# Hybrid encoder step: four split weight blocks kept in DRAM by each layer's first group and loaded whole by the later groups

## The chip, the cores and the metric

The kernel runs on one core of one Trainium2 chip. The metric is device time in microseconds (us) of one execution. The kernel before was timed three times: 2314.01 us in the median, from 2313.35 to 2318.27. One more execution was profiled; all rows of the trace come from that one.

## The reference, cut to what matters

Two layers over 2048 prompt tokens and 8 x 16 sample tokens, model width 1024. Per layer:

```python
xn = rms_norm(h, norm_g)
u = xn @ w_in                                   # 1024 x 2832
qa, ka, va, ga, qb, kb, vb, gb, ab = jnp.split(u, _split_points(), axis=-1)
# A: sliding-window attention of qa, ka, va;  B: gated linear attention of qb, kb, vb, ab
mix = jnp.concatenate([oa * jax.nn.silu(ga), ob * jax.nn.silu(gb)], axis=-1)
h = h + mix @ w_out                             # 1024 x 1024
gate = jax.nn.sigmoid(rms_norm(h, pe_norm_g) @ w_pg)
h = h + gate * (p_l @ w_pe)                     # 256 x 1024
```

All tensors are float32.

## The kernel before

The 2176 tokens are 17 tiles of 128, in five groups of 3, 4, 4, 3 and 3 tiles; the last group holds the sample tokens. Each layer goes through the groups in turn, so that the execution has ten stretches, called group 0 to group 9 here; groups 0 and 5 are the first of their layers. A group runs phase_in (projections, attention, linear attention) and then phase_out (output projection, gate, embedding).

To keep float32 accuracy, each weight and each activation is split into a high part, rounded to the type fp32r, and a low part, the rest; a product is three matmuls (lines 400 to 402). The activations of a group are split once. The weights don't stay on the chip: every group loads them all again and splits them again.

The list plan holds the weight blocks in the order of their use, group by group: kv, q, ga0, ga1, qb, kb, vb, gb, o0 to o3, then g0, e0 to g3, e3. A block of 256 columns (ga0, ga1, qb, kb, o, g) has two slots of half its 1024 rows; q, vb and gb, of 512 columns, and kv have four slots. A slot is a tile named w of 128 partitions by 2 (high, low) by 1024 values, 8 KB on each partition, 1 MB in all; five slots exist in a ring. A piece is 256 rows of 256 columns (272 for kv), 256 KB; every slot of the four blocks is filled from two pieces. For each piece SyncE issues a DMA into one of four buffers named raw (line 197), ScalarE copies raw to the high part (line 217), and VectorE subtracts the high part from raw into the low part (line 96 through a helper). There are 800 pieces in an execution, 80 for each group.

w_split emits the next piece: it takes a slot from the ring if the piece needs one and one is free, and emits the raw DMAs up to four pieces ahead. It is called while the last unit of matmuls of a block gives its slots back (freed, end=True), and ahead of units (w_ahead). The raw DMA of piece i + 4 waits for the subtraction of piece i; the copy of a piece into a reused slot waits for the last matmul that reads what was in it. All instructions of an engine run in one order that is fixed when the program is built, and a waiting instruction holds up those behind it. All weight loads, the loads of the activations, cache and state, and the outputs are issued by SyncE in one order too.

In phase_in, units of 24 matmuls go to one PSUM buffer each. For ga, qb and kb a unit is 128 columns of the weights by all tokens of the group (512 or 384); for kv, q, vb and gb it is one tile of tokens by all columns. Evictions: q by VectorE at line 470 after a sum of squares (464, 466), ga at 761 with 751 and 752 for silu, qb at 780, kb at 784, vb by ScalarE at 1070. From the start of ga on, steps of attention and linear attention (scores s at 125 and 131, softmax at 571 to 590, transposes at 637 to 640, outputs o) are put between the units. The q tiles are transposed (546) and copied by ScalarE (548) before the scores; the gate of the linear attention runs at the same time (lines 1105 to 1117, with a table load ahead of the logarithm at 1112). The end of a group's linear attention is at lines 895 to 915.

Of the kernel before, what the change touches and what calls it, by code (L numbers as in the profile page):

```python
# [8 lines left out]
F32 = mybir.dt.float32  # L9
# [37 lines left out]
def hybrid_step(ctx: ExitStack, tc: tile.TileContext, a: dict, o: dict):  # L47
    nc = tc.nc
    V, A, G, PE, SP = nc.vector, nc.scalar, nc.gpsimd, nc.tensor, nc.sync
# [4 lines left out]
    dram = ctx.enter_context(tc.tile_pool(name="dram", bufs=1, space=bass.MemoryType.DRAM))  # L54
# [40 lines left out]
    def ptt(out, in0, in1, op1, eng=None):  # L95
        (eng or G).tensor_tensor(out=out, in0=in0, in1=in1, op=op1)  # L96
# [45 lines left out]
    plan = []  # L142
    for l in range(DEPTH):
        for gi in range(len(GROUPS)):
# [8 lines left out]
            for b in range(4):  # L153
                plan.append((l, gi, f"g{b}", 8, [a["w_pg"][l, :, b]], 4, "w"))
                plan.append((l, gi, f"e{b}", 2, [a["w_pe"][l, :, b]], 2, "we"))
    RING = dict(w=5, we=2)
    pieces = []
    for bi, (_, _, _, K, srcs, ks, _) in enumerate(plan):
        for k0 in range(0, K, 2):
            c0 = 0  # L160
            for src in srcs:
                wd = src.shape[2]
                pieces.append((bi, k0 // ks, k0 % ks, c0, wd, src[:, k0:k0 + 2, :]))
                c0 += wd
    first_piece = {}
    last_piece = {}
# [6 lines left out]
    st = dict(dma=0, split=0, blk=0)  # L173
    wgate = [None]
    RAW = Z["raw"]
# [17 lines left out]
    def w_dma(upto):  # L193
        while st["dma"] < min(upto, len(pieces)):
            bi, _, _, _, wd, src = pieces[st["dma"]]
            r = w_p.tile([128, 2, wd], F32, tag="raw", name="raw", bufs=RAW)
            SP.dma_start(out=r, in_=src)
            raws[st["dma"]] = r
            st["dma"] += 1

    def w_split():
        i = st["split"]
        if i >= len(pieces):
            return False
        bi, si, kk, c0, wd, _ = pieces[i]
        _, _, _, _, srcs, ks, tag = plan[bi]
        if (bi, si) not in slots:
            if held[tag] == RING[tag]:
                return False
            held[tag] += 1  # L210
            slots[bi, si] = w_p.tile([128, 2, ks, sum(x.shape[2] for x in srcs)], F32R, tag=tag, name="w", bufs=RING[tag])
        w_dma(i + RAW)
        w = slots[bi, si]
        r = raws.pop(i)
        hi, lo = (w[:, x, kk:kk + 2, c0:c0 + wd] for x in range(2))
        with tc.issue_after(wgate[0]) if wgate[0] is not None else ExitStack():
            A.activation(out=hi, in_=r, func=ACTF.Copy)  # L217
        ptt(lo, r, hi, ALU.subtract, V)
        st["split"] += 1
        w_dma(i + 1 + RAW)  # L220
        return True

    def w_get(l, gi, nm):
        bi = st["blk"]
        assert plan[bi][:3] == (l, gi, nm), (plan[bi][:3], l, gi, nm)
        while st["split"] <= last_piece[bi]:
            assert w_split()
        st["blk"] += 1
        return Block(bi)

    def w_get_part(l, gi, nm):

        bi = st["blk"]
        assert plan[bi][:3] == (l, gi, nm), (plan[bi][:3], l, gi, nm)
        while st["split"] < first_piece[bi] + 2:
            assert w_split()
        st["blk"] += 1
        return Block(bi)

    def w_rest(w):  # L240
        while st["split"] <= last_piece[w.bi]:
            assert w_split()
# [95 lines left out]
    def prep_x(pool, l, gi, slot, out, whole=False):  # L338
# [6 lines left out]
        if whole:  # L345
            full = pool.tile([128, KD, n], F32, tag="hfull", name="hfull", bufs=1)
            for k in range(0, KD, 2):
                HQ[k // 2].dma_start(out=full[:, k:k + 2, :], in_=src[:, k:k + 2, t0:t0 + n])
                if k // 2 in WD:
                    w_dma(WD[k // 2])  # L350
# [85 lines left out]
    def phase_in(l, gi, ip, xn, mslot, S_in):  # L436
# [651 lines left out]
        for mt in range(4):  # L1088
            if mt == 3:
                with tc.issue_after(lastmm[0]):  # L1090
                    done["tail"]()
            pss.append(unit_a(mixes, ws[mt // 2], mt % 2, 0, n, pm(n) if mt < 2 else pw1(n), ks=(0, 4), end=mt % 2 == 1))
        ws.append(w_get_part(l, gi, "o2"))
        for mt in (4, 5):
            pss.append(unit_a(mixes, ws[2], mt % 2, 0, n, pw1(n), ks=(0, 4), end=mt % 2 == 1))
# [176 lines left out]
def _prepare(inputs):  # L1272
# [65 lines left out]
    for t in range(NT):  # L1338
# [18 lines left out]
             ks=(DEPTH, 128, 128), vs=(DEPTH, 128, 128), ss=(DEPTH, 8, 128, 2, 128))  # L1357
# [32 lines left out]
```

## Time and profile before

| | us |
|---|---|
| median of three runs | 2314.01 |
| lowest, highest | 2313.35, 2318.27 |
| profiled execution | 2322.44 |
| its span, first to last instruction | 2320.7 |
| mean granted TensorE clock in the span | 0.993 |

The page gives for each engine the time in which it is busy, for the whole span and in 40 slices. Matmuls overlap, and a busy stretch of TensorE (PE) may hold matmuls that run slowly; the weight loads of TensorE are listed apart (PEld). DVE is VectorE, ACT is ScalarE, POOL is GpSimd, SP is SyncE, and SPq is its DMA-issuing side. The chain that ended last follows the execution back from its last instruction, at each step to what released it. The granted clock is a share of full speed: 1.00 is 2.4 GHz, and the lower level is 1.2 GHz.

In rows by group of instructions, names are output<-input. In rows of a timeline the first number is the start in us from the span's start, the second the duration in us of the instruction or of the run of equal instructions (x2 is two of them), and brackets give the engine's idle time ahead of it and what ended that.

### The profile page before, as it was taken

To read this page: it belongs to the slowest core of one execution; us is meant where nothing else is said; L and a number is where in the kernel's file an instruction comes from. 1 tells how busy PE (TensorE), PEld (TensorE's weight loads), DVE (VectorE), ACT (ScalarE), POOL (GpSimd) and SP (SyncE) were. 2 spreads that over 40 slices of the span, in tenths; PEclk is the share of its full clock that TensorE was granted. 3 is DMA by queue.
4 is the path that set the end of the run, shared out by engine and by line. 5 is a ranking of instruction groups with operands and counts; after the bars stand their busy time and mean duration, and the time that the engine had idled before them with its cause. 6 is when DMAs were issued, how large, how long until landed. Compare 5 with 4: busy or idle time off the path is not lost.

```text
span 2320.7 us, 40960 instructions
## 1 busy us (share of the span) xinstructions
PE 2268.3 (98%) x14814; PEld 1953.6 (84%) x14814; DVE 1605.0 (69%) x3279; ACT 1272.2 (55%) x2962; POOL 671.0 (29%) x771
## 2 busy tenths in 40 slices
PE   8999999999999999999999999999999999999999
PEld 7889877887788989987988998778877888798889
DVE  7767765767567766776777677657676678677755
ACT  6555644655455645654665566445555556566533
POOL 3124322342223231413322241314412142233222
PEclk9999999999999999999999999999999999999999
DMA  5344313433154425444543543244322443264343
GB/s 159 101 150 133 107 55 119 143 105 91 55 155 120 128 85 169 147 118 127 180 128 91 171 136 90 68 128 133 114 73 74 146 146 110 85 184 146 104 131 102
DMA packets 160234, 278.93 MB, mean 120 GB/s; under 512 B 17648, under 2 KB 43632, under 8 KB 160032
## 3 DMA queue, kind: packets, MB, share of 16 engines
q1 hardware_dynamic: 159344, 275.43, 39.4%
q8 instruction: 117, 1.92, 0.3%
q10 hardware_dynamic: 688, 0.88, 0.1%
q14 instruction: 85, 0.70, 0.1%
HBM read 255.41 MB, written 20.71 MB: 119 GB/s over the span
## 4 chain that ended last, share of the span: by engine, by line
PE 83%; ACT 4%; DVE 4%; DMA 4%; issue 3%; POOL 2%; ACTq 0%; DVEq 0%; POOLq 0%; SPq 0%
PE mm L400 15%; PE mm L402 15%; PE mm L401 14%; PE pw L400 9%; PE pw L401 9%; PE pw L402 9%; PE o L131 3%; DVE w L96 2%; PE s L131 2%; PE s L125 2%; DMA raw<-in_w_pe_dram 1%; DMA raw<-in_w_out_dram 1%; PE o L125 1%; ACT gsq L895 1%; ACT w L217 1%
## 5 line engine op out<-in xcount | busy, mean ns | idle before, releaser
L96 DVE TENSOR_TENSOR w<-raw,w 128x512 fp32r<-128x512 f32 (+1 forms) x800 | 571.7, 743 | 164.6 <-ACT w L217 161.7
L217 ACT ACTIVATE w<-raw 128x512 fp32r<-128x512 f32 (+1 forms) x800 | 468.9, 627 | 271.1 <-DMA raw<-in_w_pe_dram 60.0
L96 POOL TENSOR_TENSOR ot<-gth,hst 128x384 f32<-128x384 f32 (+1 forms) x79 | 101.7, 1291 | 287.6 <-DVE gth L1189 263.4
L400 PE MATMUL mm<-B,w 128*128 128x384 f32 (+1 forms) x440 | 160.8, 365 | 1.1 <-DVE yq L470 0.8
L402 PE MATMUL mm<-B,w 128*128 128x384 f32 (+1 forms) x440 | 159.8, 363 | 0.0
L401 PE MATMUL mm<-B,w 128*128 128x384 f32 (+1 forms) x440 | 159.0, 361 | 0.0
L400 PE MATMUL pw<-mix,w 128*128 128x384 f32 (+1 forms) x424 | 153.0, 361 | 0.0
L580 ACT ACTIVATE P<-s,mx 128x192 f32<-128x192 f32 (+3 forms) x272 | 108.8, 413 | 77.5 <-DVE mx L575 71.3
L401 PE MATMUL pw<-mix,w 128*128 128x384 f32 (+1 forms) x424 | 151.2, 357 | 0.0
L402 PE MATMUL pw<-mix,w 128*128 128x384 f32 (+1 forms) x424 | 151.0, 356 | 0.0
L400 PE MATMUL mm<-A,w 128*128 128x384 f32 (+1 forms) x408 | 148.5, 364 | 2.0 <-DVE yq L470 1.8
L96 POOL TENSOR_TENSOR acc<-sq,acc 128x384 f32<-128x384 f32 (+1 forms) x60 | 74.1, 1235 | 257.1 <-ACT sq L331 257.1
L402 PE MATMUL mm<-A,w 128*128 128x384 f32 (+1 forms) x408 | 148.0, 363 | 0.0
L401 PE MATMUL mm<-A,w 128*128 128x384 f32 (+1 forms) x408 | 147.8, 362 | 0.0
L400 PE MATMUL mm<-w,A 128*128 128x512 f32 (+1 forms) x360 | 138.2, 384 | 0.0
L400 PE MATMUL mm<-w,B 128*128 128x512 f32 (+1 forms) x360 | 137.9, 384 | 0.0
L402 PE MATMUL mm<-w,B 128*128 128x512 f32 (+1 forms) x360 | 137.7, 383 | 0.0
L402 PE MATMUL mm<-w,A 128*128 128x512 f32 (+1 forms) x360 | 137.6, 382 | 0.0
L401 PE MATMUL mm<-w,A 128*128 128x512 f32 (+1 forms) x360 | 137.4, 382 | 0.0
L401 PE MATMUL mm<-w,B 128*128 128x512 f32 (+1 forms) x360 | 137.4, 382 | 0.0
L96 POOL TENSOR_TENSOR mix<-ga_t,mix 128x512 fp32r<-128x512 f32 x34 | 43.9, 1290 | 283.1 <-ACT mix L606 283.1
L1186 ACT ACTIVATE gth<-gth 128x384 f32<-128x384 f32 (+2 forms) x81 | 45.1, 560 | 125.6 <-DVE gth L1185 125.3
(325 smaller groups left out, 6367.6 us busy)
## 6 DMA issues: line engine op xcount, KB each, us to landing
raw<-in_w_in_dram SPq DMA_DIRECT2D x400, 256.0 KB, 2.9
raw<-in_w_out_dram SPq DMA_DIRECT2D x160, 256.0 KB, 3.1
raw<-in_w_pg_dram SPq DMA_DIRECT2D x160, 256.0 KB, 2.9
raw<-in_w_in_dram SPq DMA_DIRECT2D x40, 272.0 KB, 3.2
raw<-in_w_pe_dram SPq DMA_DIRECT2D x40, 256.0 KB, 3.4
hl<-in_h_dram SPq DMA_DIRECT2D x24, 192.0 KB, 3.1
hbuf<-ot SPq DMA_DIRECT2D x24, 192.0 KB, 2.1
hx<-hbuf SPq DMA_DIRECT2D x24, 192.0 KB, 3.6
```

Source lines behind the costliest of these rows:

```text
L96: (eng or G).tensor_tensor(out=out, in0=in0, in1=in1, op=op1)
L125: prev[0] = PE.matmul(**kw).ins
L131: prev[0] = PE.matmul(**kw).ins
L217: A.activation(out=hi, in_=r, func=ACTF.Copy)
L400: PE.matmul(out=out, lhsT=sh, rhs=mh, start=first and i == 0, stop=False)
L401: PE.matmul(out=out, lhsT=sh, rhs=ml, start=False, stop=False)
L402: lastmm[0] = PE.matmul(out=out, lhsT=sl, rhs=mh, start=False, stop=last and i == n).ins
L580: A.activation(out=P[:, e, p0:p0 + wd], in_=ps[:, e // 2, e % 2, :wd], func=ACTF.Exp, scale=0.125, bias=mx[:, e:e + 1], accum_out=den[:, 0 ...
L895: A.activation(out=gq, in_=po[:, h % 2, h // 2, :], func=ACTF.Square, accum_out=ss[:, h:h + 1])
L1186: ta = A.activation(out=th[:, c], in_=th[:, c], func=ACTF.Tanh, scale=0.5)
```

## The change

In the first group of each layer, the slots of ga1, qb, kb and vb (2 + 2 + 2 + 4 = 10 slots) are filled as before, and after the last subtraction of a slot SyncE stores the whole slot, both parts, to a DRAM tile: 1 MB, 8 KB in a row for each partition. In the four later groups of the layer, each of these slots is one entry in the list of pieces, of width 0; for it w_split issues one DMA of 1 MB from the DRAM tile into the slot, with no raw buffer, no copy and no subtraction. The other blocks are loaded and split in every group as before.

```diff
     RING = dict(w=5, we=2)
+
+    KEEP = [('ga1','qb','kb','vb')]
+    kept = {}
+    for bi, (l, gi, nm, K, srcs, ks, _) in enumerate(plan):
+        if gi < len(KEEP) and nm in KEEP[gi]:
+            kept[l, nm] = (gi, dram.tile([K // ks, 128, 2, ks, sum(x.shape[2] for x in srcs)], F32, name=f"k{l}{nm}"))
     pieces = []
-    for bi, (_, _, _, K, srcs, ks, _) in enumerate(plan):
+    for bi, (l, gi, nm, K, srcs, ks, _) in enumerate(plan):
+        if (l, nm) in kept and gi > kept[l, nm][0]:
+            pieces += [(bi, si, 0, 0, 0, kept[l, nm][1][si]) for si in range(K // ks)]
+            continue
         for k0 in range(0, K, 2):
...
     def w_dma(upto):
         while st["dma"] < min(upto, len(pieces)):
             bi, _, _, _, wd, src = pieces[st["dma"]]
+            if not wd:
+                st["dma"] += 1
+                continue
...
         w_dma(i + RAW)
         w = slots[bi, si]
+        if not wd:
+            SP.dma_start(out=w.bitcast(F32), in_=src)
+            st["split"] += 1
+            w_dma(i + 1 + RAW)
+            return True
         r = raws.pop(i)
...
         st["split"] += 1
         w_dma(i + 1 + RAW)
+        if kept.get((l_, nm_), (None,))[0] == gi_ and (i == last_piece[bi] or pieces[i + 1][1] != si):
+            SP.dma_start(out=kept[l_, nm_][1][si], in_=w.bitcast(F32))
         return True
```

w_get_part, which asks for the first slot of a block, asks for one entry instead of two where the block is loaded whole; it is called for o2 alone, which isn't.

## Rows read from the trace of the kernel before

**Rows 1.** The page's first part (busy time and share of the span by engine) and its fourth (the chain that ended last, by engine).

```profile
PE 2268.3 (98%) x14814; PEld 1953.6 (84%) x14814; DVE 1605.0 (69%) x3279; ACT 1272.2 (55%) x2962; POOL 671.0 (29%) x771
...
PE 83%; ACT 4%; DVE 4%; DMA 4%; issue 3%; POOL 2%; ACTq 0%; DVEq 0%; POOLq 0%; SPq 0%
```

**Rows 2.** Busy time of each engine from the first eviction of ga to the last of vb in the eight later groups, and the sum. Columns: the stretch, its length, busy us (instructions) by engine, granted clock, mean share of the DMA engines, GB/s.

```profile
271.00:351.00 80.00, 80.00 (x558) 62.25 (x558) 56.37 (x122) 43.16 (x127) 16.46 (x21) 1.00 0.23 66
...
sum 569.00, PE 568.87 PEld 463.67 DVE 411.30 ACT 318.13 POOL 117.52; mean PE 71.11 PEld 57.96 DVE 51.41 ACT 39.77 POOL 14.69
```

**Rows 3.** Timeline of TensorE in group 2, from the last units of q to the first of ga0.

```profile
528.67 0.39 PE L401 MATMUL mm<-A,w 128*128 128x512 f32 x1
528.90 0.39 PE L402 MATMUL mm<-A,w 128*128 128x512 f32 x1
...
531.99 0.50 PE L400 MATMUL mm<-A,w 128*128 128x512 f32 x1 [1.85 <-DVE yq L470]
...
533.03 0.63 PE L400 MATMUL mm<-A,w 128*128 128x512 f32 x1
533.46 0.63 PE L401 MATMUL mm<-A,w 128*128 128x512 f32 x1
```

**Rows 4.** Timeline of VectorE at the same place.

```profile
528.36 1.29 DVE L96 TENSOR_TENSOR w<-raw,w 128x512 fp32r<-128x512 f32 x2
...
530.05 1.28 DVE L96 TENSOR_TENSOR w<-raw,w 128x512 fp32r<-128x512 f32 x2
531.25 0.68 DVE L470 TENSOR_TENSOR yq<-mm,qrs 128x512 f32<-128x512 f32 x1
```

**Rows 5.** Busy time by engine behind two pauses of TensorE (groups 2 and 9) and in one (group 5), with the columns of rows 2.

```profile
532.00:540.00 8.00, 8.00 (x32) 6.43 (x33) 6.16 (x16) 4.71 (x15) 0.59 (x1) 0.79 0.22 65
...
1200.00:1204.00 4.00, 0.64 (x10) 0.48 (x8) 3.68 (x10) 3.95 (x7) 0.52 (x1) 1.00 0.51 125
...
2133.00:2140.00 7.00, 7.00 (x37) 6.68 (x35) 5.37 (x21) 2.61 (x4) 0.00 (x0) 0.76 0.26 80
```

**Rows 6.** Timeline of TensorE in group 9, at the end of q.

```profile
2129.76 0.60 PE L546 MATMUL t<-cst,yq 128*128 128x128 f32 x4
2132.59 0.40 PE L125 MATMUL s<-kT,qs 64*128 64x192 f32 x1 [2.23 <-issue]
```

**Rows 7.** Timeline of ScalarE at the same place.

```profile
2125.79 0.63 ACT L217 ACTIVATE w<-raw 128x512 fp32r<-128x512 f32 x1
...
2128.96 0.62 ACT L217 ACTIVATE w<-raw 128x512 fp32r<-128x512 f32 x1
2129.60 1.28 ACT L1112 ACT_TABLE_LOAD   x1
2130.89 1.12 ACT L1112 ACTIVATE ze<-ze,onet 128x384 f32<-128x384 f32 x2
2131.92 0.57 ACT L548 ACTIVATE qs<-t 128x512 f32<-128x512 f32 x1
```

**Rows 8.** The page's costliest groups of instructions: the two steps of a split. Behind the count stand busy us, the mean ns of one, and the idle time ahead of them.

```profile
L96 DVE TENSOR_TENSOR w<-raw,w 128x512 fp32r<-128x512 f32 (+1 forms) x800 | 571.7, 743 | 164.6 <-ACT w L217 161.7
L217 ACT ACTIVATE w<-raw 128x512 fp32r<-128x512 f32 (+1 forms) x800 | 468.9, 627 | 271.1 <-DMA raw<-in_w_pe_dram 60.0
```

**Rows 9.** The longest wait of TensorE in total: who waited for whom, us in total, times, the longest in us.

```profile
PE t L912 <- DVE on L901: 9.2, 13, 1.9
```

**Rows 10.** The answer on DMA issues: KB each, median us from issue to landing.

```profile
ckT<-in_ckT_dram SPq DMA_DIRECT2D x2, 512.0 KB, 4.9
cv<-in_cv_dram SPq DMA_DIRECT2D x2, 512.0 KB, 3.5
```

**Rows 11.** All 800 raw loads, from the view of the tile raw.

```profile
DMA to landing us min/median/max: 2.6/3.0/7.4
```

**Rows 12.** Timeline of ScalarE in group 3, a split into the last vb slot, in the second half of kb.

```profile
817.56 1.15 ACT L217 ACTIVATE w<-raw 128x512 fp32r<-128x512 f32 x2 [1.28 <-PE mm L402]
```

**Rows 13.** Timeline of TensorE at the same place: the 19th matmul of the first vb unit, the first that reads the last vb slot.

```profile
825.29 0.39 PE L400 MATMUL mm<-w,B 128*128 128x512 f32 x1
```

**Rows 14.** Waits of SyncE's DMA queue, the longest in total.

```profile
SPq L197 <- DVE w L96: 1283.7, 641, 23.1
```

**Rows 15.** The page's third part: SyncE's queue, packets, MB, the time of its packets as a share of 16 engines' span.

```profile
q1 hardware_dynamic: 159344, 275.43, 39.4%
```

**Rows 16.** The answer on DMA for 50 to 92 us of group 0: busy tenths and GB/s in 40 slices.

```profile
DMA  8799399405957400006903940004840673000036
GB/s 187 248 369 244 125 248 330 164 0 92 332 119 271 185 0 0 0 0 158 336 6 43 328 144 8 0 0 47 318 142 8 135 230 135 0 0 0 0 53 205
```

**Rows 17.** Timeline of VectorE in group 0: subtractions of weights; the last of the first row completes ga1's first slot, the second row completes kb's first slot, the fifth of the ten.

```profile
48.73 1.89 DVE L96 TENSOR_TENSOR w<-raw,w 128x512 fp32r<-128x512 f32 x3
...
61.29 0.69 DVE L96 TENSOR_TENSOR w<-raw,w 128x512 fp32r<-128x512 f32 x1
```

**Rows 18.** Busy time by engine in a stretch of group 0, with the columns of rows 2.

```profile
50.00:62.00 12.00, 12.00 (x77) 11.56 (x77) 10.56 (x26) 7.62 (x19) 3.15 (x3) 1.00 0.70 211
```

**Rows 19.** Timeline of ScalarE in group 0: pairs of w copies for the slots after those, the first and the last of four (two pairs are left out between them).

```profile
69.53 1.16 ACT L217 ACTIVATE w<-raw 128x512 fp32r<-128x512 f32 x2
...
87.54 1.16 ACT L217 ACTIVATE w<-raw 128x512 fp32r<-128x512 f32 x2
```

**Rows 20.** Timeline of SyncE in group 0: the issue of the raw load for the first copy of rows 19.

```profile
61.33 0.33 SPq L197 DMA_DIRECT2D raw<-in_w_in_dram  x1
```

More of the change, by code (lines that the diff above doesn't have):

```diff
@@ L204, in w_split @@
             return False
-        bi, si, kk, c0, wd, _ = pieces[i]
-        _, _, _, _, srcs, ks, tag = plan[bi]
+        bi, si, kk, c0, wd, src = pieces[i]
+        l_, gi_, nm_, _, srcs, ks, tag = plan[bi]
         if (bi, si) not in slots:
@@ L234, in w_get_part @@
         assert plan[bi][:3] == (l, gi, nm), (plan[bi][:3], l, gi, nm)
-        while st["split"] < first_piece[bi] + 2:
+        while st["split"] < first_piece[bi] + (2 if pieces[first_piece[bi]][4] else 1):
             assert w_split()
```

## The prediction

> **What bounds the kernel now.** I began with the first and fourth parts of the page [rows 1]: TensorE is busy for 98% of the span and holds 83% of the chain that ended last. A busy share alone can hide slow stretches, so I next asked for busy time by stage, one stretch for each of the eight later groups (1 to 4 and 6 to 9), from the first eviction of ga to the last of vb, which is where the four changed blocks are multiplied [rows 2]. TensorE is busy there for 568.87 of 569.00 us. VectorE is busy for 411.30 us and ScalarE for 318.13 us, 72% and 56%. So in these stages the splits that the change takes away lie beside matmuls, and relief of the two engines is worth nothing there by itself. What is left to win are the few places where TensorE does stand still, and the question is which of them a split causes. I looked for idle time ahead of a matmul, and found two in later groups in which the four blocks' splits stand directly ahead of the instruction that TensorE waits for.
>
> In group 2, TensorE is idle for 1.85 us until 531.99, put down to the q eviction of line 470 on VectorE [rows 3]. VectorE did that eviction at 531.25, behind four w subtractions begun at 528.36 and 530.05 [rows 4]. After that pause the granted clock is 0.79 over the next 8 us [rows 5]: it goes down to the lower of its two levels, 1.2 GHz, and comes back, and in that stretch the 512-column matmuls start 0.43 us apart where they started 0.23 us apart before [rows 3]. That is 8 x 0.21 = 1.68 us more.
>
> In group 9 the same thing has another last link. TensorE is done with the q transposes and is idle for 2.23 us until 2132.59 [rows 6]. The score products need the copy of q by ScalarE, line 548, which starts only at 2131.92, behind a row of work with four w copies in it, from 2125.79 to 2128.96, then a table load of 1.28 us and 1.12 us of logarithms [rows 7]. The clock is 0.76 over the next 7 us [rows 5], again 7 x 0.24 = 1.68 us.
>
> By the order of the pieces, the eight splits at the end of q are the second slot of ga0 (two), both slots of ga1 (four) and the first of qb (two). The last four are the ones named above, and the change takes them away in a later group.
>
> **The change part by part.**
>
> *Splits removed.* Ten slots of two pieces in eight later groups: 160 of 800. At 743 and 627 ns [rows 8] that is 119 us of VectorE and 100 us of ScalarE. By rows 2 nearly all of it is worth 0. On the path: in group 2 the four subtractions (2 x 1.29 us) stand ahead of line 470, so that it is ready before TensorE wants it, and 1.85 + 1.68 = 3.5 us go. In group 9 the four copies (0.62 to 0.63 us each, 2.5 us) go from ahead of the table load; the copy of q can then start when the transposes end, 2129.76 + 0.60 = 2130.36, takes 0.57 us and leaves a pause of some 0.6 us in place of 2.23. I take 1.6 us and the 1.68 us of clock, 3.3 us; what is late next there is the transpose itself. Sum 6.8 us. Bounds: 0, if the freed instructions only move up behind another wait, and about 10 us if pauses that I count as untouched shrink as well. The pauses at the end of a group (line 912 behind 901, 9.2 us in all) [rows 9] lie where gb and o are split, as before, and I take nothing there. Group 5 has a pause of 3.4 us at 1200 [rows 5], but it is the first group of its layer and splits everything still: 0.
>
> *Raw loads removed, whole loads added.* 160 loads of 256 KB go; 80 of 1 MB come, 84 MB for 42. A 256 KB load lands at best in 2.6 us [rows 11], 512 KB for cv in 3.5 us [rows 10]; by that step of 0.9 us per 256 KB, 1 MB lands in 2.6 + 3 x 0.9 = 5.3 us. The other end is ckT, 4.9 us for 512 KB among other transfers [rows 10], and so 2.6 + 3 x 2.3 = 9.5 us. I take 5.3, since cv too goes out during ga to vb. The load waits on SyncE for the slot that the matmuls give back, where before ScalarE waited. The tightest case is the last vb slot: its space comes free in the second half of kb, and it is read at the seventh k of the first vb unit. In group 3 the split released by that is at 817.56 and the matmul at 825.29 [rows 12, 13]: 7.7 us of cover. So 0, with 2.4 us to spare, and 1.8 us missing per group at the far end. Slots of ga1, qb and kb have a block more. The Trainium skill (DMA: Bandwidth & Descriptors, section Bandwidth) lists 6.15 us and 341 GB/s for 1 MB on another issuing path; by it the spare time would be 1.6 us and the sum the same. No run so far shows a 1 MB transfer here.
>
> *Behind SyncE's new wait* stand the raw loads of gb, the sample group's cache and state loads and the outputs. SyncE waited at those places before too: 1283.7 us on w subtractions [rows 14], and a subtraction waits for the slot in turn. The raw buffers are all empty when the vb loads are issued, so gb's first four pieces go out without a wait of their own. 0. The change also takes away a link (split i before raw i + 4), for which I count nothing.
>
> *Stores added in groups 0 and 5.* Ten of 1 MB each, 10.5 MB per layer. A store waits for the same subtraction as the raw load issued just ahead of it, so it adds no wait on SyncE; it adds traffic ahead of the raw loads that follow. While its queue moves anything it moves 275.43 MB in 39.4% of 2320.7 us, 301 GB/s [rows 15]; in one slice of 1 us with the engines 90% busy or more it moved 369 GB/s [rows 16]. A store is then 3.5 or 2.8 us. From 50 to 62 us five slots are complete (the first with VectorE's subtraction that ends at 50.6, the fifth with that which ends at 62.0 [rows 17]), with the DMA engines 0.70 busy already [rows 18]: 8.4 + 5 x 2.8 - 12 = 10.4 us are owed at 62 us at the fast end, 13.9 at the slow end. If full queues make packets overlap better, those 2.5 MB of raw loads need 6.9 us at 369 GB/s instead of 8.4, and 8.9 us are owed. The raw load issued at 61.33 [rows 20] has some 3.0 us to landing [rows 11] and is split at 69.53 [rows 19], so it has 5.2 us of spare time; the store made last at 62 is behind it, which makes 8.9 - 2.8 = 6.1 us of waiting for it. It is late by about 1 us. ScalarE and then VectorE stand for that time with other work behind them, while the slot itself is needed a block later. I take 1 us for each first group, 2 in all, between 0 and the whole of the next rival.
>
> Sum: -6.8 + 2 = -4.8 us. The profiled execution takes 2322.44 us, 1.74 more than its span and 8.43 more than the median of the runs, 2314.01. It would become 2317.6; with the same distance the median becomes 2309.2, and I say **2309 us**.
>
> **The rivals.**
>
> *A, the pauses move (no difference).* The q end is a knot of evictions, scans, a table load and splits. Only group 2 gives its 3.5 us back, group 9 waits for table load and logarithms still, or another of the eight q ends gets a pause of 2 us and its 1.7 us of clock in exchange. For it: such pauses appear in two of the later groups and not in the others with the same code, which looks like an accident of order. Net -3.5 + 2 = -1.5: about 2312.5 us, between 2309.5 and 2318.
>
> *B, the stores starve the split (slower).* Place: groups 0 and 5, between ga1 and vb. It decides where the queue stays near 301 GB/s: then 13.9 us are owed at 62 us, 10.4 ahead of the load issued at 61.33, which is 5.2 us late, with both engines behind it. Less than one 384-column unit (24 x 0.17 = 4.1 us) can be evicted late before TensorE stands; with a clock loss of 1.7 us that is 1 + 1.7, and the same at the next three pairs of pieces, up to 87.54 [rows 19]: 4 x 2.7 = 11 us per layer, 22 in all. With the gain, 2314 - 6.8 + 22 = 2329 us; with one such pause per layer 2314 - 6.8 + 5.4 = 2313, with three 2323. Against it: 369 GB/s was reached among 2 KB packets, and the copies have runs of 8 KB.
>
> *C, more comes back.* The end-of-group pauses get shorter since both engines reach gb with less owed: -10 us, 2304.
>
> **How the numbers follow.** A timed comparison of this kernel can tell about 0.2%, 4.6 us, from no change. Forecast (2305 to 2309.4, faster) 0.35; C 0.10; A 0.35, of which 0.02 slower; B 0.20, of which 0.17 slower and 0.03 within the bound. So faster 0.45, same 0.36, slower 0.19. The likeliest case alone runs from 2305 to 2311. For 8 in 10 the range takes in C to 2302, all of A, and B up to nearly three pauses per layer: 2302 to 2321.
>
> **What would show it.** Right: 640 splits; no idle time ahead of ga0's first unit in group 2; a pause under 1 us at the q end of group 9, and 1.00 of clock behind both; 1 MB loads landing in 5 to 6 us and no matmul of a later group waiting for one; raw loads in groups 0 and 5 landing up to 8 us after issue, and TensorE without a pause over 1 us there between ga and vb. Wrong: idle time ahead of a vb unit (the load's cover), w copies of group 0 that wait 5 us for a raw load (B), or the two pauses still there or elsewhere (A).

## The result and the profile after

The kernel after takes 2300.98 us in the median of five runs (2299.65 to 2301.95); the kernel before, with two more runs beside them, 2315.40 (2313.35 to 2318.27). The ratio is 0.993, with an interval of 0.9919 to 0.9941: 14.4 us less where 4.8 were forecast, and 1.0 us below the low end of the range.

The first and fifth parts of the page of the kernel after, the same lines as in [rows 1] and [rows 8]:

```profile
PE 2260.0 (98%) x14814; PEld 1949.3 (85%) x14814; DVE 1510.8 (66%) x3119; ACT 1187.7 (52%) x2802; POOL 649.6 (28%) x771
...
L96 DVE TENSOR_TENSOR w<-raw,w 128x512 fp32r<-128x512 f32 (+1 forms) x640 | 464.5, 753 | 153.0 <-ACT w L234 151.4
L234 ACT ACTIVATE w<-raw 128x512 fp32r<-128x512 f32 (+1 forms) x640 | 375.4, 627 | 219.3 <-DMA raw<-in_w_pe_dram 60.2
```

640 splits are left, as meant. VectorE is relieved by 94.2 us and ScalarE by 84.5, and what counts is neither: it is what became of TensorE. Its span is 2297.9 us in this profile (an execution of 2299.65 us) and was 2320.7. Span less busy time, its idle time, went from 2320.7 - 2268.3 = 52.4 us to 37.9, by 14.5; its busy time, for the same 14814 matmuls, went down by 8.3. Together that is 22.8 us, more than the difference of the medians, since the profiled execution of before was 7.0 us above 2315.40 and that of after 1.3 below its median. So lengths and pauses read from these two profiles overstate the gain.

**The busy time** is mostly the clock. After the first 50 us, where both kernels lose some clock (0.90 before, 0.83 after), busy time by stretch (columns of rows 2) shows one stretch below 1.00 in the kernel after:

```profile
50.00:1190.00 1140.00, 1128.02 (x7421) 972.61 (x7419) 755.43 (x1552) 592.07 (x1400) 329.32 (x383) 1.00 0.46 151
1190.00:1200.00 10.00, 8.40 (x46) 8.14 (x47) 8.75 (x27) 7.90 (x21) 0.19 (x1) 0.83 0.87 316
1200.00:2297.00 1097.00, 1083.97 (x7172) 934.39 (x7170) 710.53 (x1456) 552.64 (x1311) 301.20 (x351) 1.00 0.44 145
```

The kernel before has six: the two of [rows 5] behind the q ends of groups 2 and 9, and four more:

```profile
219.00:226.00 7.00, 7.00 (x33) 6.81 (x33) 3.08 (x6) 3.46 (x5) 3.12 (x6) 0.80 0.22 78
...
1088.00:1096.00 8.00, 6.13 (x37) 4.77 (x36) 4.03 (x10) 3.82 (x15) 1.64 (x3) 0.79 0.23 66
...
1200.00:1210.00 10.00, 6.64 (x35) 6.29 (x34) 8.79 (x29) 8.13 (x20) 0.71 (x2) 0.83 0.28 79
...
2235.00:2245.00 10.00, 8.16 (x48) 6.85 (x47) 4.48 (x10) 4.38 (x18) 2.31 (x4) 0.83 0.22 66
```

Five fewer at the 1.68 us that the prediction worked out for one are 8.4 us, most of the 9.2 by which busy time fell after the first 50 us (in those 50 us it rose by 0.9). Two of the five are the q ends. Two, at 219 and at 1088 (the end of group 4), are luck: the pause ahead of them is as long in the kernel after, as the last section shows. The fifth (2235) lies at the end of group 9, where the longest pause went from 1.84 to 1.00 us.

**The idle time** went at two kinds of places. At the q end of group 2 the transposes of the last q tile (530.48 below) now stand inside a unit of ga0 with no idle time around them, where they came at 535.97 before, behind the pause of [rows 3]; in group 9 a pause of 0.34 and one of 1.08 us are left of 2.23 [rows 6]; the second waits for a q eviction, for which TensorE waited 0.35 us before. That row of before, then TensorE's timeline of the kernel after:

```profile
2125.49 0.44 PE L400 MATMUL mm<-B,w 128*128 128x384 f32 x1 [0.35 <-DVE yq L470]
```

```profile
527.38 0.60 PE L565 MATMUL t<-cst,yq 128*128 128x128 f32 x4
...
530.25 0.39 PE L419 MATMUL mm<-A,w 128*128 128x512 f32 x1
530.48 0.60 PE L565 MATMUL t<-cst,yq 128*128 128x128 f32 x4
530.83 0.48 PE L420 MATMUL mm<-A,w 128*128 128x512 f32 x1
...
2114.36 0.40 PE L125 MATMUL s<-kT,qs 64*128 64x192 f32 x1 [0.34 <-ACT qs L567]
...
2116.36 0.44 PE L419 MATMUL mm<-B,w 128*128 128x384 f32 x1 [1.08 <-DVE yq L489]
```

The other kind of place is the end of a group's linear attention. Steps of it stand between the projections: outputs o, then sums of squares (ScalarE), a factor (GpSimd), the normed rows on (VectorE), and their transposes t<-cst,on on TensorE. TensorE's waits there, first before (the other row is in [rows 9]), then after:

```profile
PE o L125 <- ACT ke L888: 7.0, 6, 2.4
```

```profile
PE t L931 <- DVE on L920: 6.2, 9, 1.9
...
PE o L125 <- ACT ke L907: 2.9, 4, 0.8
...
PE o L125 <- DVE on L920: 0.8, 1, 0.8
```

9.2 + 7.0 = 16.2 us became 9.9. The prediction had put a zero on this place. Group 3 shows what changed there. TensorE's timeline before, then after:

```profile
878.28 0.49 PE L125 MATMUL o<-vb,at 128*128 128x128 f32 x2 [2.36 <-ACT ke L888]
...
880.60 0.66 PE L912 MATMUL t<-cst,on 128*128 128x128 f32 x4
...
883.85 0.30 PE L912 MATMUL t<-cst,on 128*128 128x128 f32 x1 [0.50 <-DVE on L901]
```

```profile
868.29 0.38 PE L125 MATMUL o<-vb,at 128*128 128x128 f32 x2
...
870.50 0.66 PE L931 MATMUL t<-cst,on 128*128 128x128 f32 x4
...
875.16 0.60 PE L931 MATMUL t<-cst,on 128*128 128x128 f32 x4
```

Between the last output o and the group's last transposes stand 12 projection matmuls before and 24 after, and both pauses are gone. No line of the diff touches these steps. But the program is built with `schedule_with_timeline_sim=True`: the order of the instructions on an engine is fixed at build by a planner that goes by its own estimate of when each instruction could run, with the splits in that estimate. The order itself has changed, and the traces show that much: TensorE runs the same 14814 matmuls in all the kernels here, and by line and names their order in e3 below, with all 800 splits, differs from that of before at 11 places, in the kernel after at 3369. That the planner moved them because splits were gone from its estimate is inferred; no trace shows the planner. I call the count of matmuls above, 12 or 24, the **distance** of a group below, and give it for groups 3 and 8, beside the length of each group (from the first eviction of kv on ScalarE to that of the next group, from each profile):

| | splits | distance in 3, 8 | group 3 | group 8 | median us |
|---|---|---|---|---|---|
| before | 800 | 12 | 203.9 | 203.3 | 2315.40 |
| after | 640 | 24 | 200.1 | 199.4 | 2300.98 |
| e1, ga1 and qb kept | 736 | 12 | 202.1 | 202.6 | 2308.26 |
| e2, kb and vb kept | 704 | 24 | 200.0 | 199.5 | 2312.72 |
| e3, stores alone | 800 | 12 | 203.9 | 203.0 | 2315.30 |
| e4, ten groups load whole | 600 | 24 | 199.3 | 199.3 | 2296.73 |
| e5, after, steps later | 640 | 12 | 203.5 | 202.8 | 2314.76 |
| e6, before, steps earlier | 800 | 12 | 204.4 | 203.4 | 2305.28 |
| e7, after, steps earlier | 640 | 26 | 200.0 | 199.7 | 2290.53 |
| e8, ga0 and gb kept too | 568 | 24 | 200.2 | 199.4 | 2302.44 |
| e9, before, attention earlier | 800 | 24 | 199.3 | 199.4 | 2304.96 |

At distance 12 the two groups take 202.1 to 204.4 us, at 24 or 26 they take 199.3 to 200.2, whatever the number of splits.

### The profile page after: what moved, and what is told of

The parts are those of the page before. It is cut to its first block, busy times and chain, and to the rows that moved or that the text cites. A ratio compares the mean times of both kernels' runs of the same rounds, so it can differ in the third digit from the quotient of the medians.

```text
span 2297.9 us, 40325 instructions
## 1 busy us (share of the span) xinstructions
PE 2260.0 (98%) x14814; PEld 1949.3 (85%) x14814; DVE 1510.8 (66%) x3119; ACT 1187.7 (52%) x2802; POOL 649.6 (28%) x771
## 4 chain that ended last, share of the span: by engine, by line
PE 84%; ACT 4%; DVE 4%; DMA 4%; issue 3%; POOL 2%; ACTq 0%; DVEq 0%; POOLq 0%; SPq 0%
PE mm L421 15%; PE mm L419 15%; PE mm L420 15%; PE pw L419 9%; PE pw L421 9%; PE pw L420 9%; PE o L131 3%; DMA raw<-in_w_pe_dram 2%; PE s L131 2%; DVE w L96 2%; PE s L125 2%; PE o L125 1%; ACT gsq L914 1%; ACT w L234 1%; PE t L131 1%
## 5 line engine op out<-in xcount | busy, mean ns | idle before, releaser
L96 DVE TENSOR_TENSOR w<-raw,w 128x512 fp32r<-128x512 f32 (+1 forms) x640 | 464.5, 753 | 153.0 <-ACT w L234 151.4
L234 ACT ACTIVATE w<-raw 128x512 fp32r<-128x512 f32 (+1 forms) x640 | 375.4, 627 | 219.3 <-DMA raw<-in_w_pe_dram 60.2
```

## The experiments

Three theories are told apart. **End of q**: the gain is that of the two q ends, as forecast, and larger there than sized. **Even relief**: each split that goes is worth something everywhere, by less work on VectorE and ScalarE. **Planned order**: the gain beyond the q ends comes from steps that stand earlier in TensorE's order. The kernel before was timed again beside the experiments: 2315.94 us (21 runs) for e1 to e4, 2316.67 (15 runs) for e5 to e8, 2316.18 (8 runs) for e9; the ratios go by these.

**e1_ga1_qb**, the blocks around the q end alone:

```diff
-    KEEP = [('ga1','qb','kb','vb')]
+    KEEP = [('ga1','qb')]
```

> Only ga1 and qb are kept and loaded whole (4 of the 10 slots, 64 of the 160 splits removed); kb and vb are split in every group as before. Theory of the end of q: the six splits of ga1 and qb that stand in the way at the end of q are what matters; without them the q transposes, and with them every step of attention and linear attention, come earlier in TensorE's order and the last steps of the group are no longer exposed. It expects two thirds of the change's gain or more: 2302 to 2306 us where before is 2315. Rival, even relief: the gain follows the number of splits removed wherever they stand: 40% of 14.4 us, 2309.5 us.

2308.26 us, ratio 0.9959 (0.9945 to 0.9973). Group 2 is shorter by 3.8 us and group 9 by 5.7, so both q ends come with these blocks; groups 3 and 8, at distance 12, give 1.8 and 0.7, and group 4 loses 1.5. The time is 2.3 us above what the end of q expected and 1.2 below the rival: the q ends are there, but not the whole gain.

**e2_kb_vb**, the other half:

```diff
-    KEEP = [('ga1','qb','kb','vb')]
+    KEEP = [('kb','vb')]
```

> Only kb and vb are kept and loaded whole (6 of the 10 slots, 96 of the 160 splits removed); ga1 and qb are split in every group as before, so that the end of q keeps its splits. Theory of the end of q: little, 0 to 4 us gained, 2311 to 2315, and the q transposes of groups 3 and 8 stand where they stood before (after 100, 130 and 160 matmuls of the projections). Rival, even relief: 60% of 14.4 us, 2306.5 us.

2312.72 us, ratio 0.9982 (0.9974 to 0.9991). The pause at the q end of group 2 is back (1.83 us). The time fits the end of q; the place doesn't: groups 3 and 8 give 3.9 and 3.8 us, all that they give in the kernel after, and these two have distance 24. That is more than the 3.2 us of the medians: groups 4 and 9 lose 2.1 and 0.9, and the lengths are compared with a profile of before that is 6.5 us above the median. Even relief, with 96 splits gone, is out by 6 us.

**e3_stores**, the stores of groups 0 and 5 with nothing loaded whole:

```diff
-        if (l, nm) in kept and gi > kept[l, nm][0]:
+        if (l, nm) in kept and gi > kept[l, nm][0] + 9:
```

> The first groups store the ten slots of each layer, and no group loads them: all 800 splits stay. This is the cost of the stores alone. The prediction's term: 1 us for each first group, 2317.4 where before is 2315.4, with w copies in group 0 about 1 us late. Its rival B: 3 us or more for each first group, 2321 or more. A third view, that the stores cost nothing, gives 2315.4.

2315.30 us, ratio 0.9994 (0.9985 to 1.0003): -3.5 to +0.7 us. The stores cost nothing that can be measured, though the raw loads do land late. All raw loads from 50 to 92 us, before, then e3:

```profile
DMA to landing us min/median/max: 2.6/2.9/3.9
```

```profile
DMA to landing us min/median/max: 2.7/4.8/7.4
```

ScalarE's idle time put down to raw loads rises there from 1.6 to 4.0 us in all, and TensorE has no idle time from 50 to 92. Busy time in that stretch of e3, with the columns of rows 2:

```profile
50.00:92.00 42.00, 42.00 (x259) 39.74 (x258) 35.83 (x86) 26.10 (x74) 8.91 (x11) 1.00 0.94 350
```

The DMA engines moved 350 GB/s for 42 us, and ScalarE was busy for 26.10 of the 42, VectorE for 35.83: the lateness ends in their slack.

**e4_no_stores**, all ten groups load the ten slots whole, with no stores but one: every slot is filled from one 1 MB area with the first slot of q, so the four blocks are multiplied by other weights than the reference's.

```diff
-        if (l, nm) in kept and gi > kept[l, nm][0]:
-            pieces += [(bi, si, 0, 0, 0, kept[l, nm][1][si]) for si in range(K // ks)]
+        if nm in KEEP[0]:
+            pieces += [(bi, si, 0, 0, 0, one.rearrange("p (x k c) -> p x k c", x=2, k=ks)) for si in range(K // ks)]
```

> All ten groups load the four blocks whole, from one 1 MB area of DRAM that a slot of q fills once at the start; nothing else is stored, and 200 of 800 splits are gone. The products of ga1, qb, kb and vb are formed with those other weights, so the results differ. Theory of the end of q: the first groups get the same relief as the later ones, and group 5's pause of 3.4 us at the end of q goes with its 1.7 us of clock; with the stores' cost of 2 us gone too it is 6 to 9 us below the changed kernel, 2292 to 2295. If stores and first groups matter little: 2298 to 2301.

2296.73 us, ratio 0.9912 (0.9898 to 0.9926), 4.3 us below the kernel after and between the two expectations. Of the lengths only groups 0 (from the start of the span) and 5 are shorter than in the kernel after by over 1 us, by 1.9 and 2.5. Group 0 goes from distance 12 to 24, and 1.7 of group 5's 2.5 us are the clock loss at 1190 in the kernel after, which this execution doesn't have. So what the first groups' own splits are worth isn't shown, and this run doesn't tell order from relief.

**e5_after_late**, the kernel after with one step of attention or linear attention in place of two behind each unit of ga:

```diff
-  pga=2, pqk=2,
+  pga=1, pqk=2,
```

> The changed kernel with one step of attention instead of two behind each ga unit. All its splits are gone as before, but in the planned order of TensorE the last linear attention step of groups 3, 5 and 8 stands 12 projection matmuls ahead of the end of the group instead of 24. Theory of order: the stages from the last vb eviction to the first o eviction of groups 3 and 8 go back from some 42 us to 47 or 48 with most of it lost in total, 3 us or more each, group 5 loses too, and the kernel is 8 to 12 us slower than the changed one, 2309 to 2313. Rival, engine relief: the freed VectorE and ScalarE keep the ends of the groups short whatever the order, 2299 to 2303.

2314.76 us, ratio 0.9992 (0.9983 to 1.0), 1.8 us above what the theory of order expected. All 160 splits are gone, and so is the gain but for 1.9 us. The q ends are as in the kernel after (no pause in group 2; 1.07 us in group 9), and groups 3 and 8 are back at distance 12 and at 203.5 and 202.8 us. TensorE's timeline in group 3 and its longest wait:

```profile
873.34 1.01 PE L931 MATMUL t<-cst,on 128*128 128x128 f32 x4 [1.53 <-DVE on L920]
874.19 0.39 PE L125 MATMUL o<-vb,at 128*128 128x128 f32 x2
...
879.66 0.50 PE L931 MATMUL t<-cst,on 128*128 128x128 f32 x2 [0.87 <-DVE on L920]
```

```profile
PE t L931 <- DVE on L920: 16.9, 14, 2.0
```

The wait for on is now 16.9 us, more than before's 9.2. With o's wait for on (2.6; that for ke doesn't occur) it is 19.5 against 16.2, on a VectorE with 160 subtractions less: relief of the engine alone doesn't shorten these waits. The run isn't the distance's alone, though. Groups 3, 5 and 8, where it falls, are 3.3, 2.7 and 3.3 us longer than in the kernel after, but groups 0, 4 and 9 lose 3.1, 1.9 and 5.9 too, with distance 12 in both kernels, more than half of it by losses of clock.

**e6_before_early**, the kernel before with four steps in place of two behind each unit of qb and kb:

```diff
-  pga=2, pqk=2,
+  pga=2, pqk=4,
```

> The kernel before, with all 800 splits, and four steps of attention instead of two behind each qb and kb unit. In the planned order the last linear attention step of groups 0, 1, 2, 6 and 7 stands 24 matmuls ahead of the end of the group instead of 12; groups 3, 4, 8 and 9 keep their order there. Theory of order: the ends of those five groups get 1 to 3 us shorter with no split removed, 2305 to 2310 where before is 2315.5. Rival, engine relief: the engines are as busy as before, so 2313 to 2318.

2305.28 us, ratio 0.995 (0.9938 to 0.9963): 11 us with no split removed. Groups 1, 2, 6 and 7 go from distance 12 to 24 and give 2.2, 4.1, 2.0 and 2.4 us, group 0 likewise 4.0; groups 3 and 8 stay at 12 and are 0.5 and 0.1 us longer. The wait of o for ke (7.0 us before) doesn't occur, while that for on is 11.2, above before's 9.2: the two have to be read together, 16.2 against 11.2. The two q ends keep their pauses (1.78 and 1.93 us). That of group 2 came without a loss of clock here and in e9, so 1.7 of that group's 4.1 us, and of its 3.7 in e9, isn't the order's.

**e7_after_early**, the same step count in the kernel after:

```diff
-  pga=2, pqk=2,
+  pga=2, pqk=4,
```

> The changed kernel with four steps behind each qb and kb unit: 24 matmuls or more in groups 0 to 3 and 5 to 8. Theory of order: another 5 to 9 us below the changed kernel, 2292 to 2296. Rival, engine relief: no more than the changed kernel, 2299 to 2303.

2290.53 us, ratio 0.9882 (0.9866 to 0.9899), the fastest version, 1.5 us below what was expected: groups 1, 2, 6 and 7 give 2.0, 2.4, 2.4 and 2.6 us on top of the kernel after. Splits and step count add up, as far as they move different groups. TensorE's longest wait is down to

```profile
PE t L931 <- DVE on L920: 4.8, 4, 1.9
```

and the wait of o for ke doesn't occur.

**e8_keep_more**, ga0 and gb kept as well, by the second group of each layer:

```diff
-    KEEP = [('ga1','qb','kb','vb')]
+    KEEP = [('ga1','qb','kb','vb'), ('ga0','gb')]
```

> The changed kernel in which the second group of each layer also stores ga0 and gb, and the last three groups load them: 36 splits fewer in each of the six last groups of the layers, 72 pieces in all replaced. Theory of order: the planned order at the ends of the groups is that of the changed kernel (24 in groups 3, 5 and 8, 12 elsewhere), so it gains little, 2297 to 2301. Rival, even relief: 72 more splits after 160 that gave 14.4 us, 2294.5.

(The expectation has a count wrong: it is 12 splits fewer in each of six groups, 72 in all, as the 568 of the table show.) 2302.44 us, ratio 0.9938 (0.9926 to 0.9951), no faster than the kernel after. Nothing is gained where the distance was 24 already. Even relief is out once more; planned order came closer, but its 2297 to 2301 is missed by 1.4 us.

**e9_before_ya0**, the test of the distance in groups 3 and 8 themselves, with all 800 splits: two waiting turns of the prompt's attention are taken out, so that its steps and those behind them are emitted sooner.

```diff
-  ya=1, yb=1,
+  ya=0, yb=0,
```

> The kernel before, all 800 splits, with the two one-step pauses of the prompt attention (counts ya and yb) set from 1 to 0, so that its steps are emitted sooner. In the planned order of TensorE the last linear-attention step of groups 1, 2, 3, 7 and 8 then stands 24 or 26 projection matmuls ahead of the group's last transposes instead of 12; in groups 4, 6 and 9 it stays at 12. Order theory (the distance decides): groups 3 and 8 fall from 203.9 and 203.3 us to about 200, groups 1, 2 and 7 by about 2 us each, group 6 stays at 261.5; in all about 13 us below before, some 2303. Rival (engine relief by the missing splits decides): no split is missing, so groups 3 and 8 stay at 203 to 204 and the time within 4 us of before, 2312 to 2320.

2304.96 us, ratio 0.9958 (0.9944 to 0.9972). Groups 3 and 8 fall to 199.3 and 199.4 us, the lengths that they have in the kernel after, with every split in place; groups 1, 2 and 7 give 2.0, 3.7 and 2.3 us, and group 6, left at 12, gives 0.9. TensorE's timeline at the end of group 3, without idle time, and its waits:

```profile
865.16 0.39 PE L125 MATMUL o<-vb,at 128*128 128x128 f32 x2
...
871.65 0.60 PE L912 MATMUL t<-cst,on 128*128 128x128 f32 x4
```

```profile
PE t L912 <- DVE on L901: 5.4, 4, 1.9
...
PE mm L400 <- DVE yq L470: 2.6, 3, 1.8
```

The wait for on has fallen by 3.8 us, that of o for ke doesn't occur, and the wait behind the q eviction is as large as before (2.6 us, 1.8 of them in group 2). So the two gains of the change can be had apart: order gives the one, missing splits the other. Groups 4 and 9, left at distance 12, were not untouched: group 4 is 4.9 us longer and group 9 1.0. Why isn't settled.

## Why the prediction was wrong

**The failed step** is this one: "The pauses at the end of a group (line 912 behind 901, 9.2 us in all) [rows 9] lie where gb and o are split, as before, and I take nothing there." It costed the removed splits by the instructions that stand behind them in the trace of before, and so took TensorE's order for fixed. It isn't: with the splits gone, steps of attention and linear attention stand elsewhere in it. By the medians, 14.4 us less the 6.4 of the q ends below leaves 8.0 us. By the two profiles, groups 3 and 8, where the distance changed, are 3.8 and 3.9 us shorter, 7.7 in all; the waits at the ends of all groups fell by 16.2 - 9.9 = 6.3. Not all of that is the distance's: in group 9, at 12 in both kernels, the waits for on fell from 4.1 to 1.9 us, of which 1.3 were gone in e3 too, with the order of before. That an earlier order does this by itself is shown by e9 for groups 3 and 8 and by e6 for groups 1, 2, 6 and 7; that missing splits hardly do without it is shown by e5 (0.5 us in each of groups 3 and 8) and e1 (1.8 and 0.7). Each of these runs moves other steps of the order as well, so what is shown is that the order decides; that this one distance does fits every row of the table, but no run moves it alone. Shown as well is that the change sets it off (e2: distance 24 in groups 3 and 8 with kb and vb alone). Why the planner moves a step in groups 3 and 8 and not in 1, 2, 6 and 7 stays open.

**Rival A** didn't come: both pauses shrank, and of the later groups only group 9 has one left at its q end. **Rival C** named the right place and sign, at -10 us, with a cause that the runs speak against: engines that "reach gb with less owed" would have kept the gain of groups 3 and 8 in e5, and e9 has it with nothing less owed.

**The q ends** were right in mechanism. Group 2: 1.85 us of pause and 1.68 of clock forecast, both gone; group length -3.7. Group 9: 1.6 us of pause forecast, 2.23 + 0.35 - 0.34 - 1.08 = 1.16 measured, since the wait for the q eviction grew by 0.7, while I had named the transpose as late next; the clock, 1.68, came in full. Sum 6.4 where 6.8 were forecast. That counts both losses of clock of this one profile of before, and they aren't certain: of the five profiles with the pause in group 2 (before, e2, e3, e6, e9) two show the loss. e2, e6 and e9 keep both pauses (1.8 to 1.9 us); e1 and e5 have no pause in group 2 and one of 1.1 us in group 9, like the kernel after. So they hang on the splits of ga1 and qb, not on the steps that e6 and e9 move. That VectorE's eviction is no longer late in group 2 can be read directly: it starts behind 1.53 us of waiting for GpSimd, with no subtraction ahead of it.

```profile
527.93 0.69 DVE L489 TENSOR_TENSOR yq<-mm,qrs 128x512 f32<-128x512 f32 x1 [1.53 <-POOL qrs L488]
```

**Group 5's pause**, taken as untouched since group 5 splits everything, is 1.69 us long where it was 3.36; but it is 2.06 in e3, which runs the same splits, so most of that difference isn't the change's.

**The stores** were forecast at 2 us, between 0 and rival B. e3 puts them at 0. Their traffic is as forecast, raw loads late by up to 3.5 us (7.4 against 3.9); the step that failed is that a load that is late by more than its spare time costs TensorE what it is late by: the copies were late (the last of the stage starts at 90.5 in e3, at 89.4 before), the slots are needed a block later, and both engines caught up. Rival B needed a queue near 301 GB/s; it ran at 350.

**The whole loads** cost nothing, as forecast. Issue to landing, of the loads and of the slowest store, and the tightest case, the last vb slot of group 3 (issue on SyncE, 19th matmul of the first vb unit on TensorE):

```profile
w<-k0vb SPq DMA_DIRECT2D x16, 1024.0 KB, 4.8
...
w<-k1qb SPq DMA_DIRECT2D x8, 1024.0 KB, 7.6
...
k0qb<-w SPq DMA_DIRECT2D x2, 1024.0 KB, 8.4
```

```profile
813.86 0.32 SPq L227 DMA_DIRECT2D w<-k0vb  x1
```

```profile
823.14 0.39 PE L419 MATMUL mm<-w,B 128*128 128x512 f32 x1
```

4.8 us for vb (5.3 forecast; worked out from steps of 0.9 us per 256 KB), 5.3 to 5.4 for ga, 6.7 to 7.6 for qb. Cover is 9.3 us with 4.5 to spare (7.7 and 2.4 forecast). The figure of the Trainium skill (DMA: Bandwidth & Descriptors, section Bandwidth), 6.15 us for 1 MB on another path, counts the busy span of the DMA engines alone; it lies inside the 4.8 to 7.6 measured here from issue to landing. No wait of TensorE is put down to one of these loads.

## What to carry to other kernels

Where the order is fixed at build, work that is taken away beside a busy engine can still go with another order on that engine: before costing "the rest stays as it is", list from the trace which chains end a stage (here output, sum of squares, factor, transpose) and how many matmuls stand between their links, and give that count a term. When a change gains more than its own waits explain, test order alone, by a step count in the old kernel, before crediting the work that went; here that test gave 11 us and, combined, a kernel some 10 us faster than the changed one. Loads that the stores made up to 3.5 us later cost nothing here, since ScalarE and VectorE between them and TensorE had slack: read that slack, not the queue alone.

## What the runs showed of the hardware that I had not expected

A pause of about 2 us doesn't always lower the granted clock. Ahead of the same matmul (line 294 before, 313 after) TensorE pauses for 2.16 us before and 2.19 us after, and over the 7 us behind it the clock is 0.80 before (the row of 219:226 above) and 1.00 after. After:

```profile
218.29 0.50 PE L313 MATMUL t<-ah,ones_r 128*128 128x512 f32 x1 [2.19 <-ACT ah L308]
```

```profile
219.00:226.00 7.00, 7.00 (x46) 6.95 (x45) 3.02 (x6) 4.89 (x7) 3.71 (x7) 1.00 0.20 66
```

The end of group 4 is another such place (clock 0.79 before, the row of 1088:1096 above, and 1.00 after), before and then after:

```profile
1090.65 1.01 PE L912 MATMUL t<-cst,on 128*128 128x128 f32 x4 [1.87 <-DVE on L901]
```

```profile
1080.97 1.01 PE L931 MATMUL t<-cst,on 128*128 128x128 f32 x4 [1.86 <-DVE on L920]
```

```profile
1081.00:1089.00 8.00, 7.05 (x49) 5.75 (x50) 3.68 (x11) 2.75 (x10) 1.66 (x3) 1.00 0.27 82
```

The pause at the q end of group 2 is a third: 1.85 us and 0.79 before [rows 3, 5], 1.78 us and 1.00 in e6:

```profile
526.00:534.00 8.00, 7.92 (x38) 6.33 (x38) 6.16 (x17) 4.90 (x16) 0.59 (x1) 1.00 0.22 68
```

So the 1.68 us is the price of a loss that happens, and one profile doesn't tell whether the next execution pays it.
